# Where a ring of weight buffers begins: 32 bytes past a multiple of 64, or at a multiple of 256

## The chip, the cores and the metric

The kernel runs on one core of one Trainium2 chip. The metric is device time of one execution in microseconds (us). Engines are named as in the profile: PE is the matrix engine (PEld its weight loads, which run beside the matmuls), DVE the vector engine, ACT the scalar engine, POOL the GpSimd engine, SP the engine that issues most transfers. SBUF is the on-chip memory, 128 partitions; a tile's address is the byte at which it starts in each partition.

## The reference

Two layers of a decoder trunk over 256 tokens of width 2048, in float32:

```
h = x
layer 0: h += recurrent_mixers(rms_norm(h)) ; h += squared_relu_mlp(rms_norm(h))
layer 1: h += dilated_attention(rms_norm(h)) ; h += squared_relu_mlp(rms_norm(h))
return rms_norm(h)

recurrent_mixers: proj = h @ w_in (2048 x 6144) -> RG-LRU group and HGRN2 group -> mixed @ w_out
dilated_attention: qkv = h @ w_qkv (2048 x 6144) -> three dilated windows, merged -> out @ w_o
squared_relu_mlp: square(relu(h @ w1)) @ w2, w1 2048 x 8192, w2 8192 x 2048
```

Nearly all arithmetic is the product of 256 rows of activations with weight matrices that are read once from HBM.

## The kernel before, in words

**Units.** The weights are read in units of 128 x 2048 float32 (1 MB, 8192 bytes in each partition). A unit is four blocks of 128 x 512, each a block of the sum over k. `units` lists them in the order in which PE uses them, and `fetch`, `reserve` and `unit` load them ahead of PE.

**Split.** PE multiplies in a float32 form of reduced precision (float32r), so each operand is split in two: a high part (the value rounded) and a low part (the rest). For the weights, `Weights.split` does it: ACT copies a raw unit into a tile `hi` (`A.copy(h, w)`, in the profile `CAST hi<-raw`), and DVE subtracts it from the raw unit (`TENSOR_TENSOR low<-raw,hi`). The low part is written over the raw unit, into the same bytes. Activations are split likewise and lie in `bufa`, `bufb`, `formx` and `formh`, high part beside low part.

**Products.** `tokens` multiplies 256 rows with a unit. For each of its four blocks and each half of the rows PE runs three matmuls of 512 columns: high activations by high weights, low activations by high weights, high activations by low weights. In the profile a row `p<-hi,bufa` has the moving operand `hi` (the weights, 512 columns that stream through) and the stationary operand `bufa` (the activations, 128 x 128, brought in by a weight load of its own). So of three wide matmuls two stream from `hi` and one from `low`. The usual order is eight matmuls on `hi`, then four on `low`:

```
parts = [(i, *p) for i in range(4) for p in ((0, hi[i]), (S, hi[i]))]
parts += [(i, 0, lo[i]) for i in range(4)]
for n, (i, at_, w_) in enumerate(parts):
    mm(ps[j], xs(i, j, at_), w_, start=opens and not n, stop=ends and n == 11)
```

With `by_k` (the first group of columns of w_in) it goes block by block, four matmuls on `hi`, then two on `low`. The gate weights alone are used the other way round (`direct`): there `hi` and `low` are stationary and `bufb` moves (`p<-bufb,hi`, `p<-bufb,low`, 256 columns). All wide matmuls stand at one line, L371 (`mm`), all transposes of 128 columns at L374 (`turn`), and most DVE and ACT work at L82 (a helper that keeps the order of an engine).

**Some units are sums.** In the MLPs and projections some units are formed from others (`combine`, `make_more`): DVE adds two raw units into a tile `s`, POOL issues transfers that add to a tile in SBUF while they write (`t<-in_w`, `s<-in_w` at POOL), and the results are split like the rest (`hi<-s`, `low<-s,hi`, `hi<-t`). Their low parts go to a slot of the ring as well.

**The ring.** Raw and low parts lie in six slots of 8192 bytes, placed by hand at the upper end of SBUF:

```
nc.alloc_sbuf_tensor("arena", [P, RING * 2048], F32, side="right")
base = nc.sbuf_top
...
return nc.alloc_sbuf_tensor_at(f"{name}{n}", [P, m], dtype, offset=base + n * 8192 + 4 * at)[:, :]
```

`RING` is 6. `raw0` to `raw5` and `low0` to `low5` are views of one slot each, with half views for units that come in halves. In the built program the ring begins at byte 180,192, which is 703 x 256 + 224, or 32 past a multiple of 64. Everything else in this list begins at a multiple of 256: the three `hi` tiles (from 91,136), `xall`, `bufa`, `bufb`, `t` and `s`, `formx` and `formh` (`formh` at 152,064). Since the slots are 8192 bytes apart and a block of 512 columns is 2048 bytes, every block of every slot starts 32 past a multiple of 64, and every block of `hi` at a multiple of 256.

**What sets the order.** A scheduler that works while the program is built, with priorities (`stream`, `urgent`) and hand-made order dependencies (`after`). A slot is loaded again when PE, DVE and ACT are done with it; `hi` has three buffers, so ACT's cast of a unit waits for PE to be done with the unit three before it.

## Time and profile before

| what | value |
|---|---|
| three runs | 2136.55, 2136.83, 2137.12 us (median 2136.83) |
| profiled execution | 2137.67 us |
| its span, first to last instruction | 2135.9 us |
| granted PE clock | 0.999 |
| PE, PEld, DVE, ACT, POOL busy | 2126.3, 1741.3, 1770.9, 1392.1, 86.2 us |
| HBM read | 505.89 MB |

Busy time is the time in which at least one instruction of an engine is under way. Matmuls are pipelined: a new one starts while the one before still runs out, so a row's mean duration (some 390 to 400 ns here) is longer than the distance from one start to the next. In rows of a timeline the first number is the start (us from the start of the span), the second the time from the first start to the last end of the instructions that the row merges, and `xN` how many these are.

### The profile page before, as it was taken

The numbers are of one execution on the slowest core, as the hardware profiler recorded it, in microseconds if no ns is written. First come the engines' busy times: TensorE is split into PE (matmuls) and PEld (weight loads), VectorE is DVE, ScalarE is ACT, GpSimd is POOL, SyncE is SP. The second block draws the span as 40 slices with busy tenths as digits, with TensorE's granted clock in tenths as the row PEclk, the third lists the DMA queues.
The fourth block names the chain that finished last, engine by engine and source line by source line (L and its number), as shares of the span: only waits on it lengthen the run. The fifth ranks groups of instructions, "written<-read, shape, count | busy, mean of one in ns | idle before, by whom it ended". The sixth has DMA issues, their size and how long they took to land.

```text
span 2135.9 us, 25187 instructions
## 1 busy us (share of the span) xinstructions
PE 2126.3 (100%) x9658; PEld 1741.3 (82%) x9658; DVE 1770.9 (83%) x1688; ACT 1392.1 (65%) x1525; POOL 86.2 (4%) x105
## 2 busy tenths in 40 slices
PE   9999999999999999999999999999999999999998
PEld 8888888888888888887888888888888888888887
DVE  7686878889788889888987787789887887987887
ACT  7576556676576567567666777676755755765764
POOL 0000000000000000000000000000000000000000
PEclk9999999999999999999999999999999999999999
DMA  9544465878878879887878777777887888788795
GB/s 352 189 168 164 162 205 184 252 247 244 247 239 278 260 225 285 253 261 241 261 237 257 208 211 234 215 232 237 261 267 245 245 257 280 234 261 245 238 305 160
DMA packets 75352, 509.63 MB, mean 239 GB/s; under 512 B 8416, under 2 KB 8800, under 8 KB 17504
## 3 DMA queue, kind: packets, MB, share of 16 engines
q1 hardware_dynamic: 60912, 413.38, 52.7%
q0 software_dynamic: 14176, 94.38, 23.1%
q8 instruction: 77, 1.26, 0.2%
q14 instruction: 43, 0.35, 0.0%
q10 hardware_dynamic: 144, 0.26, 0.0%
HBM read 505.89 MB, written 2.10 MB: 238 GB/s over the span
## 4 chain that ended last, share of the span: by engine, by line
PE 97%; DMA 2%; DVE 1%; ACT 0%; issue 0%; ACTq 0%; DVEq 0%
PE p L371 60%; PE pd L371 15%; PE po L371 14%; PE pt L371 3%; PE pl L374 2%; DMA raw<-in_w 2%; PE pl L371 2%; DVE low L82 0%; ACT hi L82 0%; PE po L437 0%; PE po L374 0%; PE pt L374 0%; PE pd L374 0%; ACT xall L82 0%; DVE nr L82 0%
## 5 line engine op out<-in xcount | busy, mean ns | idle before, releaser
L82 DVE TENSOR_TENSOR low<-raw,hi 128x2048 fp32r<-128x2048 f32 (+2 forms) x357 | 769.9, 2161 | 134.2 <-ACT hi L82 133.2
L82 ACT CAST hi<-raw 128x2048 fp32r<-128x2048 f32 (+2 forms) x357 | 641.5, 1805 | 274.4 <-PE p L371 183.2
L371 PE MATMUL p<-hi,bufa 128*128 128x512 f32 x1888 | 482.6, 395 | 0.5 <-ACT hi L82 0.4
L371 PEld LDWEIGHTS p<-hi,bufa 128*128 128x128 f32 x1888 | 351.1, 188 | 78.3 <-ACT hi L82 1.4
L82 DVE TENSOR_TENSOR low<-s,hi 128x2048 fp32r<-128x2048 f32 x123 | 281.5, 2288 | 90.9 <-ACT hi L82 90.7
L82 ACT CAST hi<-s 128x2048 fp32r<-128x2048 f32 x123 | 235.2, 1912 | 151.7 <-DVE s L82 56.9
L371 PE MATMUL p<-hi,bufb 128*128 128x512 f32 x1236 | 311.9, 393 | 0.0
L371 PEld LDWEIGHTS p<-hi,bufb 128*128 128x128 f32 x1236 | 231.0, 188 | 52.6
L371 PE MATMUL p<-low,bufa 128*128 128x512 f32 x944 | 263.5, 397 | 0.6 <-DVE low L82 0.4
L371 PEld LDWEIGHTS p<-low,bufa 128*128 128x128 f32 x944 | 176.9, 188 | 42.9 <-DVE low L82 2.8
L371 PE MATMUL p<-low,bufb 128*128 128x512 f32 x618 | 171.0, 396 | 0.0
L371 PEld LDWEIGHTS p<-low,bufb 128*128 128x128 f32 x618 | 116.0, 188 | 26.6
L82 DVE TENSOR_TENSOR s<-s,raw 128x2048 f32<-128x2048 f32 x41 | 93.7, 2286 | 21.4 <-DMA raw<-in_w 15.1
L82 DVE TENSOR_TENSOR low<-t,hi 128x2048 fp32r<-128x2048 f32 x41 | 93.7, 2284 | 15.0 <-ACT hi L82 15.0
L82 DVE TENSOR_TENSOR s<-raw,t 128x2048 f32<-128x2048 f32 x41 | 93.7, 2284 | 0.2
L371 PE MATMUL p<-hi,formx 128*128 128x512 f32 x368 | 92.4, 393 | 0.0
L371 PE MATMUL pd<-hi,bufa 128*128 128x512 f32 x352 | 89.1, 395 | 0.0
L371 PE MATMUL po<-hi,bufb 128*128 128x512 f32 (+1 forms) x348 | 87.8, 389 | 0.0
L82 ACT CAST hi<-t 128x2048 fp32r<-128x2048 f32 x41 | 78.6, 1917 | 13.6 <-PE po L371 6.8
L371 PEld LDWEIGHTS p<-hi,formx 128*128 128x128 f32 x368 | 68.6, 188 | 15.2
L371 PEld LDWEIGHTS pd<-hi,bufa 128*128 128x128 f32 x352 | 65.4, 188 | 14.4
L371 PEld LDWEIGHTS po<-hi,bufb 128*128 128x128 f32 x348 | 65.0, 188 | 14.9
(328 smaller groups left out, 2727.1 us busy)
## 6 DMA issues: line engine op xcount, KB each, us to landing
raw<-in_w SPq DMA_DIRECT2D x210, 1024.0 KB, 6.8
raw<-in_w_in SPq DMA_DIRECT2D x44, 1024.0 KB, 4.9
raw<-in_w_qkv SPq DMA_DIRECT2D x42, 1024.0 KB, 5.9
t<-in_w SPq DMA_DIRECT2D x32, 1024.0 KB, 7.5
t<-in_w POOLq DMA_DIRECT2D x32, 1024.0 KB, 10.3
s<-in_w POOLq DMA_DIRECT2D x32, 1024.0 KB, 10.4
raw<-in_w_o SPq DMA_DIRECT2D x14, 1024.0 KB, 5.2
raw<-in_w_out SPq DMA_DIRECT2D x16, 512.0 KB, 4.5
```

The costliest lines, as they stand in the source:

```text
L82: i = call(*args, **kw)
L371: chain[:] = [after(T.matmul(*args, **kw), chain)]
L374: chain[:] = [after(T.transpose(out_, in_, ident), chain)]
```

## The change

The allocation of the ring is made larger by as many bytes as lie between its place and the multiple of 256 below it. The allocation sits against the upper end of SBUF, so it then begins at such a multiple; the bytes stay unused behind the last slot.

```
-    nc.alloc_sbuf_tensor("arena", [P, RING * 2048], F32, side="right")
+    spare_bytes = (nc.sbuf_top - RING * 8192) % 256
+    nc.alloc_sbuf_tensor("arena", [P, RING * 2048 + spare_bytes // 4], F32, side="right")
     base = nc.sbuf_top
```

`spare_bytes` is 224, and the ring begins at 179,968 = 703 x 256 instead of 180,192. All views of the slots move down by 224 bytes; no other tile has another address. On every engine the built program has the same instructions in the same order, with the same operands, DMA queues included.

## The prediction

> **What bounds the kernel now.** I read the page first, its busy times and the chain that ended last, then who PE waited for.

> ```profile
> PE 2126.3 (100%) x9658; PEld 1741.3 (82%) x9658; DVE 1770.9 (83%) x1688; ACT 1392.1 (65%) x1525; POOL 86.2 (4%) x105
> ...
> PE 97%; DMA 2%; DVE 1%; ACT 0%; issue 0%; ACTq 0%; DVEq 0%
> ```
> ```profile
> PE po L437 <- DVE e L82: 1.1, 1, 1.1
> PE p L371 <- DVE low L82: 0.4, 2, 0.2
> PE p L371 <- ACT hi L82: 0.4, 1, 0.4
> ```

> PE is under way for all but 9.6 of 2135.9 us, and 97% of the chain is PE. It waits for others for 1.9 us in all, 1.1 of them at the very start. So the time is the number of matmuls times the distance from one start to the next. Whatever changes that distance changes the time; whatever changes DVE, ACT or a transfer does not, as long as PE is fed.

> **How many matmuls touch the ring.** The same view of the whole span, taken once for the instructions that read or write `low` and once for `hi`, gives after the PE time the number of matmuls:

> ```profile
> 0.00:2136.00 2136.00, 808.82 (x2930) 549.36 (x2930) 1184.87 (x564) 1.00 0.76 239
> ```
> ```profile
> 0.00:2136.00 2136.00, 1476.87 (x5860) 1089.44 (x5860) 1184.87 (x564) 989.05 (x564) 1.00 0.76 239
> ```

> 2930 read `low`, that is the ring; 40 of these are narrow (32 with `low` stationary, below, and 8 of 256 columns), so 2890 stream 512 columns out of the ring. Twice as many, 5780, stream 512 columns out of `hi`, which lies at multiples of 256 already. The two kinds use the same activations, the same output banks and the same instruction, so the trace of before holds both placements side by side.

> **The distance from start to start, by placement.** First a stretch of the opening, where four matmuls on `hi` and two on `low` alternate (timeline of PE, starts in the first column):

> ```profile
> 11.81 1.07 PE L371 MATMUL p<-hi,bufa 128*128 128x512 f32 x4
> 12.72 0.63 PE L371 MATMUL p<-low,bufa 128*128 128x512 f32 x2
> 13.19 1.07 PE L371 MATMUL p<-hi,bufa 128*128 128x512 f32 x4
> 14.10 0.63 PE L371 MATMUL p<-low,bufa 128*128 128x512 f32 x2
> ```

> Four on `hi` take 12.72 - 11.81 = 0.91 us, 227.5 ns each; two on `low` take 13.19 - 12.72 = 0.47 us, 235 ns each. Here the stationary operands of the two `low` matmuls are the same as those of the first two on `hi`, so it is not the weight load. The durations of single matmuls say the same at 1 ns (smallest, median, largest; then a short window of the opening in which only matmuls on `hi` that follow others on `hi` run):

> ```profile
> L371 PE MATMUL p<-hi,formh x272: 389/389/398, 358.4 to 2023.7; 128*128 128x512 f32 x136
> L371 PE MATMUL p<-low,bufb x618: 392/396/398, 314.1 to 2122.5; 128*128 128x512 f32 x155
> ```
> ```profile
> L371 PE MATMUL p<-hi,bufa 128*128 128x512 f32 x2 | 0.6, 389 | 0.0
> ```

> A duration is the distance plus some 162 ns of run-out (397 against 235), so 389 stands for 227 ns: that is PE's pace on `hi` when nothing disturbs it. A matmul on `low` costs 7 to 8 ns more, over the whole span and whatever the stretch. Now the usual order of the MLPs, eight on `hi`, four on `low`:

> ```profile
> 505.93 2.00 PE L371 MATMUL p<-hi,bufb 128*128 128x512 f32 x8
> 507.77 1.10 PE L371 MATMUL p<-low,bufb 128*128 128x512 f32 x4
> 508.71 2.00 PE L371 MATMUL p<-hi,bufb 128*128 128x512 f32 x8
> 510.55 1.10 PE L371 MATMUL p<-low,bufb 128*128 128x512 f32 x4
> 511.48 2.00 PE L371 MATMUL pd<-hi,formh 128*128 128x512 f32 x8
> ```

> The four on `low` take 0.94 and 0.93 us, 234 ns each. The eight on `hi` behind them take 1.84 us, 230 ns each, 0.024 us more than eight times 227: something of the four is still paid by the matmuls that follow.

> Is it the start address, or something else about `low`? The gate weights answer in part. There `hi` and `low` are the stationary operand, and the weight loads are:

> ```profile
> L371 PEld LDWEIGHTS p<-hi,formh x272: 187/188/189, 358.2 to 2023.5; 128*128 128x128 f32 x136
> ...
> L371 PEld LDWEIGHTS p<-bufb,hi x32: 187/188/188, 96.4 to 180.4; 128*128 128x128 f32 x32
> ```
> ```profile
> L371 PEld LDWEIGHTS p<-bufb,low x16: 192/192/192, 96.8 to 180.5; 128*128 128x128 f32 x16
> ```

> Same shape, same type, same moving tile; a load from the ring takes 192 ns in all 16, one from `hi` never over 188. `formh` lies high in SBUF (byte 152,064) at a multiple of 256 and loads in 188 ns, so height alone is not it. A read that starts 32 past a multiple of 64 and costs one step more fits both: 7 ns on 2048 bytes, 4 ns on 512. I take the start address as the cause.

> **The change part by part.** It removes and adds no instruction and no wait, and moves nothing; it gives 2890 moving reads, 32 narrow or stationary ones, every raw load and every DVE and ACT access to the ring another start.

> *Moving reads of `low`*: 7 ns (396 against 389, 234 against 227) x 2890 = 20 us, all on the path that sets the end.

> *The matmuls on `hi` behind them*: 5780 / 8 = 722 runs of eight. Some follow transposes instead, after which `hi` is slow as well:

> ```profile
> 64.85 0.60 PE L374 MATMUL po<-tab__213,tk 128*128 128x128 f32 x4
> 65.21 2.09 PE L371 MATMUL p<-hi,bufa 128*128 128x512 f32 x8
> 67.14 1.09 PE L371 MATMUL p<-low,bufa 128*128 128x512 f32 x4
> ```

> (1.93 us for the eight instead of 1.84.) The 9658 - 8790 = 868 other matmuls come mostly in groups of four or eight, so 110 to 220 runs follow one; I take 150, which keep their cost. The other 570 x 0.024 us = 14 us. This term is bounded by 0 (the slow start of `hi` has another cause, as behind transposes) and 17 (all 722 runs). I take 14, since runs of `hi` that follow `hi` go at 227.

> *Weight loads from the ring*: 32 x 4 ns = 0.1 us, hidden beside the matmuls.

> *DVE, ACT and the loads.* Rows with and without the ring:

> ```profile
> L82 DVE TENSOR_TENSOR low<-raw,hi 128x2048 fp32r<-128x2048 f32 x317 | 724.3, 2287 | 132.4 <-ACT hi L82 131.6
> ...
> L82 DVE TENSOR_TENSOR s<-raw,t 128x2048 f32<-128x2048 f32 x41 | 93.7, 2284 | 0.2
> ...
> L82 DVE TENSOR_TENSOR bufb<-bufb,raw 128x1024 f32<-128x1024 f32 x7 | 8.5, 1218 | 0.0
> L82 DVE TENSOR_TENSOR bufb<-bufb 128x1024 f32<-128x1024 f32 x7 | 8.5, 1214 | 0.0
> ```
> ```profile
> L82 ACT CAST hi<-raw 128x2048 fp32r<-128x2048 f32 x317 | 602.6, 1906 | 272.0 <-PE p L371 181.7 <-PE pd L371 30.0 <-PE po L371 24.3
> ...
> L82 ACT CAST hi<-t 128x2048 fp32r<-128x2048 f32 x41 | 78.6, 1917 | 13.6 <-PE po L371 6.8 <-PE pt L371 2.5 <-issue 2.4
> ```
> ```profile
> raw<-in_w SPq DMA_DIRECT2D x210, 1024.0 KB, 6.8
> ...
> t<-in_w SPq DMA_DIRECT2D x32, 1024.0 KB, 7.5
> ```

> DVE gains 3 to 8 ns in some 560 instructions (2 to 4 us of 1771), ACT loses up to 11 ns in a cast (4 us of 1392), and a load into an aligned tile is not shorter than one into the ring. All of it lies beside PE, in engines that idle; I cost it at nothing. What covers it is PE's work on units already split.

> *Where PE is not far ahead of its feed*, part of the gain is lost. The chain that ended last, in order of time, shows three such places, and PE's timeline what follows the second:

> ```profile
> 632.67 13.28 DMA raw<-in_w
> ...
> 970.52 13.60 DMA raw<-in_w
> ...
> 1682.12 12.74 DMA raw<-in_w
> ```
> ```profile
> 986.15 2.11 PE L371 MATMUL p<-hi,bufa 128*128 128x512 f32 x8 [0.42 <-ACT hi L82]
> 988.47 1.20 PE L371 MATMUL p<-low,bufa 128*128 128x512 f32 x4 [0.21 <-DVE low L82]
> ```

> A slot comes free at 970.5, its load lands 13.6 us later, and PE waits for the cast and the subtraction behind it. The 15.6 us from the slot to PE's first use do not shrink; PE's work in that time shrinks by 34 / 2136 = 1.6%, 0.25 us, and is lost there. The loss is local, because the chain starts with a slot that PE itself frees. If three times as many places are that tight, it is 10 x 0.25 = 2.5 us, which I take, between 0.8 (nothing beyond today's waits on DVE and ACT) and 8, for the stretch before such a place in which DVE is nearly full:

> ```profile
> 967.00:985.00 18.00, 18.00 (x83) 14.75 (x82) 17.14 (x18) 13.56 (x16) 1.73 (x2) 1.00 0.97 279
> ```

> (DVE 17.14 of 18 us; over the span it is 83%, so it doesn't become the bound.)

> **Sum.** 2137.67 - 20 - 14 + 2.5 = 2106 us against the profiled execution; the median of the runs is 0.84 lower, and I take 2106 as the time, rounding against the gain.

> **Rivals.** *Only the low matmuls gain*: the slow start of `hi` stays, as it does behind transposes. For it speaks that I have a row for the delay behind transposes and none that says what drives it; against it, that runs of `hi` settle at 227 when left alone. 2137 - 20 + 2.5 = 2119 us.

> *The address is not the cause, nothing changes*: `low` is slow because the ring is being loaded and rewritten all the time, or because of where the slots lie above `formh`. Against it: 234 to 235 ns in the opening and in the MLPs alike, while the loads differ, and 192 ns without exception. 2137 us. [...]

> *DVE takes over*: the tight stretches, 15 to 20 us each with DVE at 95%, spread backwards until most of the gain is waited away. It decides if DVE has no idle time over some 100 us; its 132 us of waits for ACT in the row above are spread, which speaks against. 2128 us.

> *Slower*: with all tiles at multiples of 256, the moving read of `low`, the weight load and the writes of ACT and DVE start on like lines at once and hold each other up. The one row in which an aligned source is slower is ACT's cast, 1917 against 1906, 0.6%; 0.6% of 235 ns on 2890 matmuls is 4 us: 2141 us. It decides from 1.5 ns on a `low` matmul. Against it: `hi` and `bufa` are at multiples of 256 both, and run at 227.

> **How the numbers follow.** Both terms pay: 66%, 2099 to 2114 (2099 with 17 for `hi`, the whole 20 and no new waits). Only `low` pays: 15%, 2114 to 2124. DVE takes most: 4%. No change: 11%. Slower: 4%. A measurement of this kernel tells 0.2% (4 us) from no change, so faster is 85%, same 11%, slower 4%. The range that leaves out 2 in 10 runs from 2099 to 2122.

> **What would show it.** In the profile after, the rows `p<-low,...` should have a median of 389 to 390 instead of 396, a `low` run of four should take 0.91 us and a run of eight on `hi` behind it 1.82; the loads `p<-bufb,low` 188 ns; PE's waits for `hi` and `low` should grow from 0.8 to some 3 us, at the places behind the three loads above first of all. If `low` stays at 396, the address was not the cause; if `low` falls and the first matmuls on `hi` stay at 230, the second term was wrong; if PE's waits grow by over 10 us, the feed was.

## The result and the profile after

Four runs of the changed kernel took 2105.09 to 2106.52 us, median 2105.75; four of the kernel before, on the same chip, 2136.55 to 2137.12, median 2136.75. The ratio is 0.9855, with a 95% interval from 0.9838 to 0.9872: 31 us or 1.45% faster, against a forecast of 2106.0. The profiled execution after took 2105.09 us. Its page shows the span, busy times and shares of the chain:

```profile
span 2103.3 us, 25187 instructions
...
PE 2093.1 (100%) x9658; PEld 1739.0 (83%) x9658; DVE 1768.7 (84%) x1688; ACT 1392.3 (66%) x1525; POOL 86.3 (4%) x105
...
PE 97%; DVE 1%; DMA 1%; ACT 0%; issue 0%; DVEq 0%; ACTq 0%
```

PE has as many matmuls as before and is busy for 33.2 us less (2126.3 to 2093.1), while the span fell by 32.6 (2135.9 to 2103.3). DVE and ACT, which also read and write the ring, changed by -2.2 and +0.2 us. So the gain lies in PE's pace. The same two views of the whole span as in the prediction, of the instructions on `low` and then of those on `hi` (first after the length: PE's time, and the number of its instructions), divide it:

```profile
0.00:2103.00 2103.00, 790.40 (x2930) 548.84 (x2930) 1184.17 (x564) 1.00 0.77 242
```
```profile
0.00:2103.00 2103.00, 1462.65 (x5860) 1088.23 (x5860) 1184.17 (x564) 991.38 (x564) 1.00 0.77 242
```

`low` went from 808.82 to 790.40, 18.4 us less, and `hi`, whose address did not change, from 1476.87 to 1462.65, 14.2 us less. Together that is 32.6 us of the 33.2 that PE's busy time fell by; the span fell by 0.6 us less than PE's busy time, because PE stood idle for 10.2 us instead of 9.6. Durations of single matmuls on each of the two (smallest, median, largest; line numbers are one higher than before, because the change adds a line):

```profile
L372 PE MATMUL p<-low,bufb x618: 387/389/402, 309.6 to 2090.0; 128*128 128x512 f32 x155
...
L372 PE MATMUL p<-low,formh x136: 389/389/389, 355.1 to 1993.8; 128*128 128x512 f32 x136
```
```profile
L372 PE MATMUL p<-hi,formh x272: 389/389/389, 353.2 to 1992.9; 128*128 128x512 f32 x136
```

The median on `low` fell from 396 to 389, and on `hi` the spread from 389 up to 398 is gone: all 272 matmuls of the row take 389 ns. PE's timeline at the place of the MLPs that the prediction showed:

```profile
498.28 1.98 PE L372 MATMUL p<-hi,bufb 128*128 128x512 f32 x8
500.09 1.07 PE L372 MATMUL p<-low,bufb 128*128 128x512 f32 x4
501.00 1.98 PE L372 MATMUL p<-hi,bufb 128*128 128x512 f32 x8
502.81 1.07 PE L372 MATMUL p<-low,bufb 128*128 128x512 f32 x4
```

From start to start, eight on `hi` take 1.81 us (1.84 before) and four on `low` 0.91 (0.94): 2.72 us for a block of twelve instead of 2.77.

### The profile page after: what moved, and what is told of

Read it like the earlier page. It is cut to its first block, busy times and chain, and to the rows that moved or that the text cites. A ratio compares the mean times of both kernels' runs of the same rounds, so it can differ in the third digit from the quotient of the medians.

```text
span 2103.3 us, 25187 instructions
## 1 busy us (share of the span) xinstructions
PE 2093.1 (100%) x9658; PEld 1739.0 (83%) x9658; DVE 1768.7 (84%) x1688; ACT 1392.3 (66%) x1525; POOL 86.3 (4%) x105
## 4 chain that ended last, share of the span: by engine, by line
PE 97%; DVE 1%; DMA 1%; ACT 0%; issue 0%; DVEq 0%; ACTq 0%
PE p L372 60%; PE pd L372 15%; PE po L372 14%; PE pt L372 3%; PE pl L375 2%; PE pl L372 2%; DMA raw<-in_w 1%; DVE low L83 1%; PE po L438 0%; ACT hi L83 0%; PE po L375 0%; DVE y L83 0%; DVE s L83 0%; DVE formx L83 0%; PE pd L375 0%
## 5 line engine op out<-in xcount | busy, mean ns | idle before, releaser
L372 PE MATMUL p<-low,bufa 128*128 128x512 f32 x944 | 257.1, 390 | 0.3 <-DVE low L83 0.2
L83 DVE TENSOR_TENSOR s<-s,raw 128x2048 f32<-128x2048 f32 x41 | 93.7, 2286 | 22.5 <-DMA raw<-in_w 16.1
L83 DVE TENSOR_TENSOR low<-t,hi 128x2048 fp32r<-128x2048 f32 x41 | 93.6, 2284 | 13.9 <-ACT hi L83 13.9
L83 DVE TENSOR_TENSOR s<-raw,t 128x2048 f32<-128x2048 f32 x41 | 93.6, 2284 | 0.2
L83 ACT CAST hi<-t 128x2048 fp32r<-128x2048 f32 x41 | 78.6, 1918 | 12.6 <-PE po L372 6.3
L372 PE MATMUL po<-hi,bufa 128*128 128x512 f32 x292 | 76.3, 393 | 0.6 <-DVE y L83 0.5
## 6 DMA issues: line engine op xcount, KB each, us to landing
raw<-in_w SPq DMA_DIRECT2D x210, 1024.0 KB, 7.0
raw<-in_w_in SPq DMA_DIRECT2D x44, 1024.0 KB, 4.9
raw<-in_w_qkv SPq DMA_DIRECT2D x42, 1024.0 KB, 6.0
t<-in_w SPq DMA_DIRECT2D x32, 1024.0 KB, 7.2
t<-in_w POOLq DMA_DIRECT2D x32, 1024.0 KB, 10.2
s<-in_w POOLq DMA_DIRECT2D x32, 1024.0 KB, 10.2
raw<-in_w_o SPq DMA_DIRECT2D x14, 1024.0 KB, 5.3
```

The costliest lines, as they stand in the source:

```text
L83: i = call(*args, **kw)
L372: chain[:] = [after(T.matmul(*args, **kw), chain)]
```

## The experiments

All twelve kernels are the changed kernel with other addresses; none leaves work out, and on every engine the order of instructions is the same. "Offset" below is the start of the moving operand less the start of the stationary one, modulo 256; every block of 512 columns of a tile has that of the tile, since blocks are 2048 bytes apart. In the changed kernel `hi`, the ring, `bufa`, `bufb`, `formx` and `formh` all start at multiples of 256, and all offsets are 0. Before, the ring started at 224, so that every wide matmul on `low` had an offset of -32. Each time below is a median, each ratio is to the kernel before on the same chip, with its 95% interval. The quoted passages under an edit are what was expected of its runs before they were made, in the order of the runs.

Three theories matter below. The prediction's: a read is slow by its own start (in the expectations A, with a step of 64 bytes; B and A2, with a step of 256). A second, called S in the expectations: the two tiles that stream, `hi` and the ring, must start alike. A third, R: the moving and the stationary operand must start alike.

**The ring alone at other starts (e1, e2, e3).** The first three put the ring 64, 128 and 32 bytes past a multiple of 256, with all other tiles as in the change:

```
-    base = nc.sbuf_top
+    base = nc.sbuf_top + 64     # e1; 128 in e2, 32 in e3
```

> The ring begins 64 past a multiple of 256. Theory A (a moving read pays one step more when it starts off a multiple of 64): median of the matmuls that stream low 389 ns, time 2105 to 2107 us as with the change. Theory B (the step is 256 bytes): 395 to 397 ns and 2134 to 2138 us. Rival C (the bytes behind the ring or its lower place, not its start, made the gain): 389 ns and 2106 us here too, told from A by the next run but one.

> The ring begins 128 past a multiple of 256. Theory A (step of 64): 389 ns on low, 2105 to 2107 us. Theory B (step of 256): 396 ns, 2134 to 2138 us. If 64 past is slow and 128 past is fast, the step is 128.

> The ring begins 32 past a multiple of 256, with the same 224 bytes allotted behind it as the change has (192 of them still unused). Theory A: 396 ns on low, 2134 to 2138 us, all of the gain gone. Rival C (the spare bytes or the place): 389 ns, 2106 us.

They took 2138.44 us (1.0005, 0.9995 to 1.0014), 2134.56 (0.9982, 0.9973 to 0.9991) and 2146.15 (1.004, 1.0025 to 1.0055). So a ring at a multiple of 64 gains nothing, one at a multiple of 128 next to nothing, and one 32 past a multiple of 256 is slower than before. Theory A missed e1 and e2, for which it had 2105 to 2107 us, and e3 is 8 us above the highest that was expected of it (2138). The spare bytes and the lower place are there in all three and are not what helped. Of e1, one row each of `low` and of `hi`:

```profile
L372 PE MATMUL p<-low,formh x136: 394/396/398, 360.4 to 2025.3; 128*128 128x512 f32 x136
```
```profile
L372 PE MATMUL p<-hi,formh x272: 388/390/398, 358.6 to 2024.3; 128*128 128x512 f32 x136
```

At 64 past a multiple of 256 `low` is as slow as it was at 32 past a multiple of 64 (medians of 396 ns both). The prediction's "one step more" of a 64-byte kind fell here; a step of 256 was still open.

**The stationary operand moved (e4).** `bufa` is allocated 64 bytes wider and used from its 32nd byte; what is allocated behind it (`bufb`, `hi`, `formx`, `formh`, `t`, `s`) moves up by 64 bytes. The ring stays at a multiple of 256.

```
-    bufa = act.tile([P, KB, 2 * S], F32R, name="bufa")
+    bufa = act.tile([P, KB * 2 * S + 16], F32R, name="bufa")[:, 8:8 + KB * 2 * S].rearrange("p (k s) -> p k s", k=KB)
```

> The change is kept and the stationary operand is moved instead: bufa begins 32 past a multiple of 64, and with it every one of its 128 x 128 blocks, which 3680 wide matmuls load. If a stationary read off a multiple of 64 costs 4 ns in the weight load but hides beside the matmul before it (my reading of the loads of 192 ns in the profile before): loads p<-hi,bufa 192 instead of 188 ns, matmuls 389, time 2105 to 2107 us. If weight loads are on PE's path: 4 ns x 3680 = 15 us more, 2120 us. If the start of a stationary operand does not matter at all: loads 188, 2105 to 2107 us.

It took 2142.92 us (1.0026, 1.0016 to 1.0036): the ring is where the change puts it, and the whole gain is gone. None of the expectations had that (by the rows of before, 3954 wide matmuls use `bufa`, not the 3680 that they reckon with), and since `hi` had moved too, the run alone didn't say why. Its rows tell it afterwards. For `low` (start 0) and `hi` (start 64), each with `bufa` (32) and with `formh` or `bufb` (64):

```profile
L372 PE MATMUL p<-low,bufa x944: 389/396/502, 5.9 to 2042.8; 128*128 128x512 f32 x189
...
L372 PE MATMUL p<-low,formh x136: 394/394/397, 362.3 to 2030.2; 128*128 128x512 f32 x136
```
```profile
L372 PE MATMUL p<-hi,bufa x1888: 387/396/588, 4.9 to 2041.9; 128*128 128x512 f32 x189
L372 PE MATMUL p<-hi,bufb x1236: 387/389/478, 314.4 to 2126.7; 128*128 128x512 f32 x177
```

The same `hi` tiles are slow against `bufa` (offset 32, 396 ns) and fast against `bufb` (offset 0, 389 ns); `low`, which differs from both, is slow against all (394 to 396). No property of one tile alone does that.

**Everything moved alike (e5, e6).** A constant tile at the low end is made 64 (e5) or 32 bytes (e6) wider, so that all later tiles move up by as much, and the ring by the same:

```
-    base = nc.sbuf_top
+    base = nc.sbuf_top + 64                                   # 32 in e6
-    spare = cst.tile([P, 1], F32, name="spare")
+    spare = cst.tile([P, 17], F32, name="spare")[:, :1]       # 9 in e6
```

> Every tile and the ring begin 64 bytes further up: all operands of the wide matmuls start 64 past a multiple of 256, and none differs from another. After the runs with the ring at 64 and 128 (no gain) my theory of a step of 64 has fallen. Theory R (it counts whether the operands that PE reads start alike, modulo 256): 2104 to 2108 us, matmuls on hi and low 389 ns. Theory A2 (each operand that starts off a multiple of 256 costs by itself): slower than before the change, 2140 to 2160 us, hi and low both over 393 ns.

> As the run before with 32 bytes instead of 64: all operands start 32 past a multiple of 256, which is no multiple of 64 either. Theory R: 2104 to 2108 us, 389 ns. Theory A2: 2140 to 2170 us. If only this one of the two is slow, lines of 64 bytes count after all, beside the likeness.

2106.45 us (0.9856, 0.9841 to 0.9871) and 2105.57 (0.9853, 0.9838 to 0.9868): the whole gain, with no operand of the wide matmuls at a multiple of 256. Of e6, where each starts 32 past one:

```profile
L372 PE MATMUL p<-low,formh x136: 389/389/389, 355.3 to 1993.4; 128*128 128x512 f32 x136
```
```profile
L372 PE MATMUL p<-hi,formh x272: 389/389/389, 353.5 to 1992.5; 128*128 128x512 f32 x136
```

A read that starts 32 past a multiple of 64 takes the 389 ns of the changed kernel. The start itself is not the cause; whether the operands start alike is.

**Which must be alike (e7, e8).** In e7 the three `hi` tiles alone move up by 64 bytes, between two small gaps; in e8 the ring moves with them, so that both moving operands have an offset of 64 to all stationary ones.

```
+    pool("gap0").tile([P, 16], F32, name="gap0")
     whi = pool("whi", 3)
+    pool("gap1").tile([P, 48], F32, name="gap1")
...
-ONES = 240
+ONES = 176
...
-    base = nc.sbuf_top          # e8 only
+    base = nc.sbuf_top + 64     # e8 only
```

> The change is kept, and only the three hi tiles start 64 past a multiple of 256; ring and stationary operands at multiples. Theory R: the 5780 matmuls on hi are now those that start unlike their stationary operand, slower than before: 2150 to 2180 us. Theory S (hi and low must start alike, whatever the stationary operand): about as slow as the ring alone off, 2134 to 2150 us.

> Both moving operands, hi and the ring, start 64 past a multiple of 256, the stationary operands at multiples. Theory S (moving operands must start like each other): 2104 to 2108 us. Theory R in its form moving against stationary: all 8670 wide matmuls are off, 2150 to 2180 us. Theory A2: the same 2150 to 2180, told from R by the run with all operands at 64.

e7 took 2132.59 us (0.998, 0.997 to 0.9989), 1.4 us below the lowest that S gave it and far below what R gave it; by itself it doesn't decide between them. e8 took 2120.5 (0.9923, 0.9906 to 0.9939). e8 is where S and R part: `hi` and the ring start alike, by S the full gain should be there, and half of it is missing. Its rows:

```profile
L374 PE MATMUL p<-low,formh x136: 388/392/394, 357.0 to 2009.3; 128*128 128x512 f32 x136
```
```profile
L374 PE MATMUL p<-hi,formh x272: 388/392/394, 355.2 to 2008.3; 128*128 128x512 f32 x136
```

Both are at 392 instead of 389. The direction is R's, but R's size (2150 to 2180 us) was far too high: an offset of 64 costs 3 ns in the median, less than the 7 that -32 cost before. And R alone has no account of the two times together: e7, where two of three wide matmuls have the offset of 64, is 12 us slower than e8, where all have it. Only e7 has a difference between `hi` and the ring, and it seems that this costs something as well, or makes the other cost more; no run here separates the two.

**Both kinds in one kernel (e9).** A tile of 64 bytes more ahead of `formx`, `formh`, `t` and `s` gives these a start of 64. Only matmuls with `formx` and `formh` as the stationary operand then have an offset, -64; those with `bufa` and `bufb` keep 0.

```
-ONES = 240
+ONES = 256
```

> With the change, everything behind the small tile nr begins 64 bytes further up: the stationary tiles formx and formh, and t and s, start 64 past a multiple of 256, while the stationary tiles bufa and bufb, hi and the ring stay at multiples. Theory R (PE's moving and stationary operand must start alike): inside this one kernel the chains of twelve on formx and formh (1920 of 8670 wide matmuls) slow down by some 27 ns a chain as in the run with both moving operands at 64, the chains on bufa and bufb stay at 2.72 us; time 2108 to 2112 us. Theory S (only hi and low must be alike): no chain changes, 2105 to 2107 us. Theory T (a tile that DVE and ACT read, s or t, must start like the ring): all chains of the MLPs slow down alike.

2119.34 us (0.9913, 0.9899 to 0.9928); R had said 2108 to 2112, S no change against the changed kernel, and a fourth theory, T (a tile that DVE and ACT read must start like the ring), that all chains of the MLPs become slow. The rows on `low`:

```profile
L372 PE MATMUL p<-low,bufb x618: 388/389/398, 310.3 to 2104.1; 128*128 128x512 f32 x155
L372 PE MATMUL p<-low,formx x184: 392/394/427, 398.9 to 2085.0; 128*128 128x512 f32 x184
...
L372 PE MATMUL p<-low,formh x136: 392/394/398, 355.9 to 2007.3; 128*128 128x512 f32 x136
```

The same six slots, at one address, take 389 ns against `bufb` and 394 against `formx` and `formh`. That shows within one execution what neither S nor T has: the start of the stationary operand counts, against that of the moving one. It doesn't show that this pair alone counts (e7 and e8). PE's timeline shows what R missed in size:

```profile
503.28 1.98 PE L372 MATMUL p<-hi,bufb 128*128 128x512 f32 x8
505.10 1.07 PE L372 MATMUL p<-low,bufb 128*128 128x512 f32 x4
506.00 2.03 PE L372 MATMUL pd<-hi,formh 128*128 128x512 f32 x8
507.87 1.09 PE L372 MATMUL pd<-low,formh 128*128 128x512 f32 x4
508.80 2.00 PE L372 MATMUL p<-hi,bufb 128*128 128x512 f32 x8
510.64 1.07 PE L372 MATMUL p<-low,bufb 128*128 128x512 f32 x4
```

The eight on `hi` with `formh` take 1.87 us from start to start, 234 ns each. The eight with `bufb` behind them, which have no offset, take 1.84, and only then, the four on `low`, 0.91 again. The delay is carried over to matmuls that follow, as it was before from `low` to the next eight on `hi` (1.84 us): in the averages of this trace the first six of such eight are 2 to 9 ns late, and the last two are at full pace (some 227).

**How much by which offset (e10, e11).** As e8, with 128 and with 32 bytes instead of 64:

```
-    base = nc.sbuf_top
+    base = nc.sbuf_top + 128                        # 32 in e11
+    pool("gap0").tile([P, 32], F32, name="gap0")    # 8 in e11
     whi = pool("whi", 3)
+    pool("gap1").tile([P, 32], F32, name="gap1")    # 56 in e11
...
-ONES = 240
+ONES = 176
```

> hi and ring 128 past a multiple of 256, stationary operands at multiples. If the likeness counts modulo 256 (theory R): slow as with 64, 2115 to 2135 us. If it counts modulo 128 between moving and stationary operand: 2105 to 2107 us.

> hi and ring 32 past a multiple of 256, stationary operands at multiples. Theory R: slow, 2115 to 2135 us; how far tells whether the size goes with the distance (then less than the 2120 us at 64) or not. If 64 bytes is the unit of the likeness, 32 costs nothing: 2105 to 2107 us.

2149.17 us (1.0052, 1.0037 to 1.0067) and 2155.47 (1.008, 1.0063 to 1.0097): with an offset of 128 or 32 on all wide matmuls the kernel is slower than before. Both are well above the 2115 to 2135 us that R had given them: it had the direction and not the size. e11 is the slowest of all. The row on `hi` of e11:

```profile
L374 PE MATMUL p<-hi,formh x272: 393/395/397, 361.4 to 2041.0; 128*128 128x512 f32 x136
```

Distances from start to start, averaged in each trace over the matmuls of 512 columns with the named stationary operand (those followed by another start within 260 ns):

| offset | where | ns from start to start |
|---|---|---|
| 0 | `formh`, changed kernel, `hi` and `low` | 226.8, 226.7 |
| 64 | `formh`, e8, `hi` and `low` | 228.8, 229.2 |
| 128 | `formh`, e10, `hi` and `low` | 232.6, 232.4 |
| 32 | `formh`, e11, `hi` and `low`; `bufa`, e4, `hi` | 233.3, 233.3; 233.3 |
| -64 | `formh`, e9, `hi` and `low`; `formh`, e4, `low` | 233.3, 233.0; 233.3 |
| -32 | `formh`, before, `low`; `bufa`, e4, `low` | 233.9; 233.1 |

Among these only 0 gives the full pace (226.8 and 226.7 ns), and the cost doesn't grow with the distance (229 at 64, 233.3 at 32). Where one kernel mixes two offsets, the table doesn't add up: in e1, with `hi` at 0, `low` at 64 takes 233.8 ns (229.2 in e8), and in e7, with `hi` at 64, `low` at 0 takes 229.9 and `hi` 230.7 (228.8 in e8).

**The identity of the transposes (e12).** Runs of `hi` behind transposes stayed slow after the change (below). The transposes' operand `tab` starts at 192; e12 moves it to 0 and leaves the activations, `hi` and the ring at multiples of 256.

```
+    pool("gap").tile([P, 48], F32, name="gap")
     act = pool("act")
...
-    spare = cst.tile([P, 1], F32, name="spare")
+    spare = cst.tile([P, 17], F32, name="spare")[:, :1]
...
-ONES = 240
+ONES = 176
```

> With the change, the identity matrix (in tab_), which is the moving operand of the transposes and starts 192 past a multiple of 256, is moved to a multiple, so that it starts like its stationary operands; the tiles from xall to hi move up by 256. If theory R holds for the transposes too and they are bound by their moving read: 544 of them and what follows them gain up to 3 ns each, 1 to 2 us, 2103.5 to 2105 us. If the weight load of float32 (140 ns in their rows, distance 109) binds them: no change, 2105 to 2107 us.

2105.41 us (0.9847, 0.9832 to 0.9862), the changed kernel's time. The 81 runs of eight behind transposes take 1.93 us on average, as in the changed kernel, so moving `tab` to a multiple of 256 did nothing for them; what makes them slow stays open.

## Why the prediction was right, and where it was not

*PE bounds the kernel, and the pace is what counts*: right; 32.6 of the 33.2 us that PE's busy time fell by are its time on `low` and `hi`, and the span fell by 32.6.

*Moving reads of `low`, 20 us*: 18.4 by the view over the span. The forecast took 7 ns for each of 2890, and that is what the typical run of four gained: 936 to 907 ns from start to start (medians of 690 runs), 7.25 ns for each. The sum is smaller, 18.4 / 2930 = 6.3 ns for each, in part because the last matmul on `low` ahead of transposes took 231 ns before and 232 after (medians of 87), and in part because some runs hold the stalls named below.

*Matmuls on `hi` behind them, 14 us*: 14.2 by the view for all of `hi`. Right, although it had only the place in the order to go by. From start to start 571 runs of eight follow `low` directly (the forecast had 570), and they fell from 1.838 to 1.815 us on average, 12.9 us in all (the median by the 24 ns of the forecast). *Those behind transposes keep their cost*: nearly; the 81 of them took 1.931 us on average before and 1.925 after. One of them, after the change (1.91 us for the eight; 1.94 at the same place before):

```profile
491.95 1.03 PE L375 MATMUL pl<-tab__213,y 128*128 128x128 f32 x8
492.74 2.07 PE L372 MATMUL pd<-hi,formh 128*128 128x512 f32 x8
494.65 1.07 PE L372 MATMUL pd<-low,formh 128*128 128x512 f32 x4
```

*DVE, ACT and the loads, nothing*: right. The ring's subtraction and cast after (busy us, mean ns), then the median time of a load from issue to landing:

```profile
L83 DVE TENSOR_TENSOR low<-raw,hi 128x2048 fp32r<-128x2048 f32 x317 | 724.1, 2286 | 119.7 <-ACT hi L83 118.6
```
```profile
L83 ACT CAST hi<-raw 128x2048 fp32r<-128x2048 f32 x317 | 604.6, 1912 | 243.0 <-PE p L372 167.5 <-issue 37.7 <-PE pd L372 10.0
```
```profile
raw<-in_w SPq DMA_DIRECT2D x210, 1024.0 KB, 7.0
```

DVE took 2287 before and takes 2286, ACT 1906 and 1912, a load 6.8 and 7.0 us; all of it is beside PE.

*Tight places, 2.5 us lost*: too much. PE's waits after:

```profile
PE po L438 <- DVE e L83: 1.1, 1, 1.1
PE p L372 <- ACT hi L83: 0.7, 1, 0.7
PE po L372 <- DVE y L83: 0.5, 1, 0.5
PE p L372 <- DVE low L83: 0.4, 2, 0.2
```

On `hi` and `low` PE waits 1.1 us, 0.8 before, and on `y` 0.5 that wasn't there: 0.8 us more in all, where the forecast had 2.5. The place whose timeline it showed did as it said: the wait for the cast grew from 0.42 to 0.68 us, by the 0.25 that PE's work ahead of it shrank. These rows count only time in which PE had run out, and a matmul that starts late within the run-out of the one before doesn't show in them. From start to start, taking all wide matmuls on `hi` and `low` that follow others of these by over 255 ns, behind the opening, the time beyond 227 ns adds up to 3.1 us before, at seven places, and to 4.4 after, at eight and one very short one: 1.4 us more. So the term was too large by one to two us. Its lower bound, 0.8, was misread too: waits that are there before the change cost nothing more after it, and the bound should have been 0.

*The sum*: the terms come to 34 - 2.5 = 31.5 us, and the profiled executions differ by 32.6 (2137.67 to 2105.09). That the median of the runs, 2105.75, lies within 0.3 us of the forecast is luck in part: the profiled execution was 0.84 above the median before and is 0.66 below it after.

*"I take the start address as the cause"*: this is the step that failed, though the time came out. What failed is the inference from "32 past a multiple of 64" to a read that is slow by itself: a ring at 64, which is a multiple of 64, gained nothing (e1, 2138.44 us), and with every operand 32 past a multiple of 256 the gain is whole (e6, 2105.57). It should have been the start relative to the stationary operand's. Before the change the ring was off a multiple of 256 and all else that the wide matmuls read was at one, so both readings gave the same number for a ring at a multiple of 256. That the change moved it there, and not just to the next multiple of 64, is why a wrong cause gave a right time, and that was luck. e5 and e6 parted them (gain with no operand at a multiple of 256), e4 and e9 show it tile against tile. The support that the prediction took from the weight loads was misread. It said that loads from the ring would fall from 192 to 188 ns. After:

```profile
L372 PEld LDWEIGHTS p<-bufb,hi x32: 187/192/192, 94.5 to 177.5; 128*128 128x128 f32 x32
```
```profile
L372 PEld LDWEIGHTS p<-bufb,low x16: 188/192/192, 94.8 to 177.6; 128*128 128x128 f32 x16
```

Those from `low` stayed at 192 and those from `hi`, which did not move, rose to 192. So a longer record of a load marks neither a slow start nor a slower kernel here.

*The rivals.* Only `low` gains (2119): refuted by `hi`'s 14.2 us. DVE takes over (2128): refuted by the waits above. No change (2137): it did not come, but its doubt, whether something else about the ring than its own start makes it slow, was sounder than the reasons against it: in e6 all operands start 32 past a multiple of 64, and the pace is full (389 ns, 2105.57 us). Slower (2141), by like starts that collide: the reverse holds, since like starts are the fast case (2105.75 us).

**What stays open.** That unlike starts cost pace (229 to 234 ns from start to start instead of 226.7), and that the delay is carried over to the next matmuls (1.84 us for eight in e9 instead of 1.81), is shown; why is not. In the traces of before and after, the load of a wide matmul's stationary operand starts some 3 ns after the matmul ahead of it and takes 188 to 192. It would fit that a matmul and the load beside it hold each other up when their starts differ; that is a guess of the author's, and no run here shows it. e9 speaks against the simplest form of it. At 99 places there a matmul on `low` whose own operands start alike has the load of `formx` or `formh` beside it, which differs from it by 64 bytes: it takes 225.8 ns, and only the next, the first with an offset of its own, takes 235.9. So the delay doesn't show in the matmul beside which the unlike weights are loaded; whether it shows one matmul late is open. Nor do the runs say why -64 costs more than 64, or why a mixture costs more than a single offset (e7 against e8). That 256 is enough is shown: in the changed kernel the ring starts at an odd multiple of 256 (703 x 256) and the stationary operands at even ones (`formh` at 594 x 256), and `low` runs at full pace (226.7 ns); 128 is not enough, by e10 (232.6 and 232.4 ns, 2149.17 us).

## What to carry to other kernels

Where PE bounds a kernel, compare the distance from start to start of like matmuls by the names of both operands, the moving and the stationary one; some ns among thousands of matmuls can be a per cent of the time (1.45% here), and no wait shows them (PE waited 1.9 us for others before the change and 2.7 after). In matmuls like these, give all tiles that PE reads together starts that are alike modulo 256 (2105.41 to 2106.45 us here, against 2119.34 to 2155.47 with unlike ones), and mind that widening one tile moves all those behind it. When an alignment is the suspect, move one tile alone, and then all of them together: only the second run tells an address from a difference of addresses.
